# Moving loads against their products in a decoder step: the convolution's input loads and the modulation's weight loads

## The chip, the cores and the metric

One core of one Trainium2 chip. The metric is the device time of one execution in microseconds (us); where several executions of a kernel are shown, their median counts. Engines: TensorE (PE) multiplies, VectorE (DVE), ScalarE (ACT) and GpSimd (POOL) work on elements, SyncE (SP) and POOL issue most transfers.

## The reference, cut to what matters

One layer of a decoder for 256 prompt tokens and 8 x 8 sample tokens (T = 320 tokens in all), in float32. What the change touches is the modulation by a vector c per sequence (6 x 2048 columns) and the convolution of width 31.

```python
ada = silu(c) @ w_ada + b_ada                       # 9 sequences x (6 x 2048)
sh1, sc1, g1, sh2, sc2, g2 = split(ada, 6)
h = layer_norm(x) * (1 + sc1) + sh1
proj = h @ w_in                                     # 2048 -> 7168: u_s, u_c2, gates
y_s = s5_scan(u_s)                                  # state-space branch
br_s = (gelu(y_s) @ w_s5_val) * sigmoid(gelu(y_s) @ w_s5_gate)
u_c = u_c2[:1024] * sigmoid(u_c2[1024:])
v = depthwise_conv(u_c, conv_w, width=31) + conv_b  # convolution branch
br_c = silu(layer_norm(v)) @ w_conv_pw
mix = (g_s * br_s + g_c * br_c) @ w_out
x = layer_norm(ALPHA * x + g1 * mix)
x = layer_norm(ALPHA * x + g2 * moe(layer_norm(x) * (1 + sc2) + sh2))
```

## The kernel before, in words

The program is traced once and a planner (`schedule_with_timeline_sim`) orders each engine's queue when it is built: an instruction's place in the program is its priority, and an instruction that stands further back may go first where the engine would else be idle. On the chip every queue runs in the order so made, and each instruction waits for what it needs.

The stages in time: the first modulation parts with the layer norm and the first 768 columns of `w_in` (until about 182 us), the rest of `w_in`, the products with `w_conv_pw`, `w_s5_val`, `w_s5_gate` and `w_out` (until about 1090 us), the routing, then the experts.

The main products, `gemm` (L551), go by units. A unit is one load of 128 x 1024 weights (512 KB, issued on SP, L557) into one of the four buffers with the tag `raw`, a split of it into a high half (`whi`, ACT, L542) and a low half (`wlo`, DVE, L543), and 24 products of 320 columns (PE, output `acc`; all products stand at line 188, that of the helper). The buffer is free when the low half is made. `run_main` (L920) runs them one ahead: it traces the load of unit n+1, then the products of unit n, then lets the side work go on. Units of interest are counted from the first one behind the 768 columns: 4 units for the rest of u_s, 32 for u_c2, 64 for the gates, then 16 for `w_conv_pw` and 32 for `w_s5_val` and `w_s5_gate`.

Side work is written as generators that yield a cost, and `Side.give` (L582) runs them while their debt is positive. After each main unit `side` (the state-space branch, `s5`) gets 2100, `cside` (the convolution, `conv`, from the first unit of the gates on) gets 1900, and `ada_rest` (the later modulation) gets 1.0.

`conv` (L856) works in 16 blocks, two for each of 8 groups of 128 channels: one of 256 prompt columns, one of 64 sample columns. A block loads four tiles (142 or 151 KB each, issued on POOL, L865, into the free ends of the tiles `s5S` and `s5T`) that hold four shifted copies of the input from the DRAM buffer `up_d`, then runs 64 products into `cv` with the taps in `wide`, which POOL makes once per group (L860), and an activation writes `vf` (L878). The four tiles exist once, so the loads of a block have to wait for the products of the one before.

`ada_set` (L292) makes 1024 columns of the modulation: for each of 8 pairs of rows of `w_ada` it loads two tiles of 512 KB (`ada_load`, issued on SP, L279, in turn) and runs four products into `adp` (eight instructions of PE each time). The tiles come from the same four `raw` buffers, and until the gates' projection begins every second one of most turns from three more (`rawu`, `rawc`). A pair's two buffers are free when its products are done. `ada_rest` runs six such sets (48 pairs) with a cost of 1.3 per yield beside the main units.

Of the kernel before, what the change touches and what calls it, by code (L numbers as in the profile page):

```python
# [19 lines left out]
D = 2048  # L20
# [128 lines left out]
def bc(ap, shape):  # L149
    return ap.to_broadcast(shape)  # L150


def build(tc, A, O):
# [24 lines left out]
    def s5p(name="s5p"):  # L178
        return pp.tile([128, 512], F32, name=name, tag="s5p", bufs=2)

    def tpp(name="tpp"):
        return pp.tile([128, 512], F32, name=name, tag="tpp", bufs=1)

    def stg(name="stg", shape=(128, T), dt=F32):
        return pa.tile(list(shape), dt, name=name, tag="stg", bufs=7)

    def mm(out, l, r, a, b, skip=True):
        return PE.matmul(out, lhsT=l, rhs=r, start=a, stop=b, skip_group_check=skip)  # L188
# [39 lines left out]
    def raw_tile():  # L228
        return pa.tile([128, 1024], F32, name="raw", tag="raw", bufs=4)
# [33 lines left out]
    def four(ops):  # L263

        lead = mm(*ops[0])
        with tc.issue_after(lead.ins), tc.high_priority(offset=3000):
            for x in ops[1:]:
                mm(*x)
# [8 lines left out]
    def in_turn(o, i):  # L277
        with tc.issue_after(turn[0]) if turn else contextlib.nullcontext():
            turn[:] = [SY.dma_start(out=o, in_=i).ins]  # L279

    def ada_load(cols, k):

        i = next(begun) % 8
        raw = more[i // 2] if i % 2 and i < 7 and len(more) else raw_tile()
        if cols[1] == cols[0] + 512:
            in_turn(raw, w_ada[:, k, cols[0]:cols[0] + 1024])
        else:
            for a, c in enumerate(cols):
                in_turn(raw[:, 512 * a:512 * a + 512], w_ada[:, k, c:c + 512])
        return raw  # L290

    def ada_set(cols):  # L292


        ps = pp.tile([128, 512], F32, name="adp", tag="adp", bufs=1)
        for k in range(0, KT, 2):
            raws = [ada_load(cols, k + h) for h in range(2)]
            four([(ps[64 * a + 32 * h:64 * a + 32 * h + 32, :], scT[:, k + h, :], raws[h][:, 512 * a:512 * a + 512],
                   k == 0, k == KT - 2) for h, a in ((1, 1), (0, 0), (0, 1), (1, 0))])
            yield  # L300
            yield
        es = [stg("ae")[:, :256] for i in range(2)]
        for i, e in enumerate(es):
            S.copy(e, ps[:, 256 * i:256 * i + 256])
        yield
        tp = tpp()
        for i in range(4):
            mm(tp[:, 64 * i:64 * i + 64], es[i // 2][:, 128 * (i % 2):128 * (i % 2) + 128], pair, True, True)
        tv = tp[:, :256].rearrange("p (i a s) -> p a i s", i=4, a=2)
        for a, c in enumerate(cols):  # L310
            f = c // 128
            tt(ada[:, f:f + 4, :], tv[:, a, :, :NS], bc(bT[:, f:f + 4, None], [128, 4, NS]), op=OP.add)
        yield
# [309 lines left out]
    for q in range(4):  # L623
        for i, _ in enumerate(ada_set([D + 512 * q, 512 * q])):
            if q == 0:
                if i == 2:
                    x_load()
                    taps()
                if i == 3:
                    bias_rows()  # L630
                    next(norm)
                if 6 <= i < 15:
                    next(norm, None)
                    next(norm, None)
                setup.give(800)
            else:
                if i % 4 == 3 and i < 16:
                    k_outer(4 * q - 4 + i // 4)
                setup.give(1100)
# [216 lines left out]
    def conv():  # L856


        for c in range(8):
            gt(wide, bc(cwS[:, c, :, :, None], [128, 4, 8, 32]), bc(oneh[:, None, None, :], [128, 4, 8, 32]), op=OP.mult)  # L860
            for t0, n, o0, m in ((0, CW - 3 + SEQ, 0, SEQ), (PS, NB * PB - 2, SEQ, NB * TS)):
                xs = [spare[k][:, 1280 + 304 * i:1584 + 304 * i] for k in "TS" for i in range(2)]
                for j, x in enumerate(xs):
                    v = up_d[c, 32 * j:32 * j + 32, t0:t0 + n]
                    GP.dma_start(out=x[:, :n], in_=bass.AP(v.tensor, v.offset, [[1, 4]] + list(v.ap)))  # L865
                yield 3500
                ps, lead = s5p("cv"), None
                for r in range(8):
                    rows = slice(0, 128 if r < 7 else 96)
                    for j in (3, 0, 1, 2):  # L870
                        x = xs[j][rows]
                        if o0:
                            x = x.rearrange("p (b t) -> p b t", b=NB)[:, :, 4 * r:4 * r + TS]
                        else:
                            x = x[:, 4 * r:4 * r + SEQ]
                        with tc.issue_after(lead.ins) if lead else contextlib.nullcontext():
                            lead = mm(ps[32 * j:32 * j + 32, :m], wide[rows, j, r, :], x, r == 0, r == 7)
                S.activation(vf[:, c, o0:o0 + m], ps[:, :m], AF.Identity, bias=vT[:, 8 + c:9 + c])  # L878
                yield 2000

    def conv_norm():
        yield 3000
# [64 lines left out]
    def chain(*gs):  # L947
        for g in gs:
            yield from g
# [29 lines left out]
    def steps(g, cost):  # L979
        for _ in g:  # L980
            yield cost

    ada_rest = Side(steps(chain(*[ada_set([p * D + 1024 * i, p * D + 1024 * i + 512])
                                  for p in (2, 4, 3) for i in range(2)]), 1.3))
    g2s = ada_g2()
    ada_last = Side(steps(g2s, 2.4))
# [8 lines left out]
    for i in range(4):  # L995
        run_main([gemm(w_in, 1024 + 256 * i, KT, *hh, ev_ua), gemm(w_in, 2048 + 256 * i, KT, *hh, ev_ub)], SD, ada_rest,
                 (lambda: side.g.append(s5())) if i == 0 else None)
    more.clear()
    run_main([gemm(w_in, 3072 + 256 * i, KT, *hh, ev_g) for i in range(16)], SD, ada_rest,
             lambda: cside.g.extend((conv(), conv_norm())))  # L1000


# [118 lines left out]
    xr, late = {}, []  # L1121
# [630 lines left out]
    fins, fx, late, lt = {}, [], {}, {}  # L1752
# [250 lines left out]
    cols = ke[:, E_N:E_N + 32]  # L2003
# [280 lines left out]
```

## Time and profile before

| what | value |
|---|---|
| median of three runs | 1654.14 us (1652.2 to 1662.36) |
| the profiled execution | 1669.45 us, its span 1667.7 us |
| PE busy | 1471.1 us, 88% of the span |
| DVE busy | 878.4 us, 53% |
| ACT busy | 551.4 us, 33% |
| POOL busy | 248.2 us, 15% |
| mean granted clock of PE | 0.942 |
| moved by DMA | 447.39 MB, 268 GB/s |

The profile is that of one execution, with every time counted from the start of its span; "idle" of an engine is put down to what ended it. An arrow <- in a wait says who was waited for, in a transfer what is read. "PEclk" is the granted share of PE's full clock.

### The profile page before, as it was taken

The numbers are of one execution on the slowest core, as the hardware profiler recorded it, in microseconds if no ns is written. First come the engines' busy times: TensorE is split into PE (matmuls) and PEld (weight loads), VectorE is DVE, ScalarE is ACT, GpSimd is POOL, SyncE is SP. The second block draws the span as 40 slices with busy tenths as digits, with TensorE's granted clock in tenths as the row PEclk, the third lists the DMA queues.
The fourth block names the chain that finished last, engine by engine and source line by source line (L and its number), as shares of the span: only waits on it lengthen the run. The fifth ranks groups of instructions, "written<-read, shape, count | busy, mean of one in ns | idle before, by whom it ended". The sixth has DMA issues, their size and how long they took to land. (4 is left out here: it accounts for less than half of the span.)

```text
span 1667.7 us, 28096 instructions
## 1 busy us (share of the span) xinstructions
PE 1471.1 (88%) x10731; PEld 1023.4 (61%) x10731; DVE 878.4 (53%) x1724; ACT 551.4 (33%) x960; POOL 248.2 (15%) x419
## 2 busy tenths in 40 slices
PE   4777978998899899989899999988879998969894
PEld 1444967877677777878788988866523332323431
DVE  4744347764834754698345645555531543424365
ACT  1321433342223223632243433323231423232534
POOL 3020212124222220111100100000200000010013
PEclk9886999999999999999899999999999998989997
DMA  9897999779769975876577654567799899999992
GB/s 256 304 312 251 270 270 250 237 190 268 197 200 250 208 199 182 221 231 222 178 253 239 201 161 147 173 209 267 306 403 413 335 413 411 413 356 411 411 412 101
DMA packets 214899, 447.39 MB, mean 268 GB/s; under 512 B 23811, under 2 KB 134067, under 8 KB 206732
## 3 DMA queue, kind: packets, MB, share of 16 engines
q1 hardware_dynamic: 179572, 395.65, 68.3%
q0 software_dynamic: 29168, 43.15, 12.0%
q10 hardware_dynamic: 6016, 6.70, 1.3%
q8 instruction: 87, 1.43, 0.4%
q14 instruction: 56, 0.46, 0.1%
HBM read 425.53 MB, written 21.77 MB: 268 GB/s over the span
## 5 line engine op out<-in xcount | busy, mean ns | idle before, releaser
L543 DVE TENSOR_TENSOR wlo<-raw,whi 128x1024 fp32r<-128x1024 f32 (+1 forms) x196 | 239.8, 1224 | 308.8 <-ACT whi L542 301.1
L542 ACT CAST whi<-raw 128x1024 fp32r<-128x1024 f32 (+1 forms) x196 | 202.2, 1032 | 390.9 <-PE acc L188 253.2
L188 PE MATMUL acc<-h_hi,whi 128*128 128x320 f32 x864 | 276.9, 325 | 5.1 <-ACT whi L542 3.0
L188 PE MATMUL acc<-h_lo,whi 128*128 128x320 f32 x864 | 272.7, 318 | 0.0
L188 PE MATMUL acc<-h_hi,wlo 128*128 128x320 f32 x864 | 261.9, 321 | 6.9 <-DVE wlo L543 6.9
L188 PEld LDWEIGHTS acc<-h_hi,whi 128*128 128x128 f32 x864 | 168.6, 196 | 30.0 <-issue 13.0
L188 PE MATMUL up<-ring,xg 128*32 128x512 f32 x1344 | 176.3, 613 | 8.4 <-PEq L2199 6.5
L188 PEld LDWEIGHTS acc<-h_hi,wlo 128*128 128x128 f32 x864 | 162.9, 194 | 22.7 <-DVE wlo L543 9.4
L188 PEld LDWEIGHTS acc<-h_lo,whi 128*128 128x128 f32 x864 | 168.1, 195 | 3.6 <-issue 1.4
L188 PE MATMUL adp<-raw,scT 128*32 128x512 f32 x636 | 119.0, 685 | 19.4 <-DMA raw<-in_w_ada 19.3
L188 PE MATMUL pd<-ring,aT 128*32 128x512 f32 (+1 forms) x688 | 100.9, 695 | 5.2 <-DVE aT L1872 5.2
L188 PEld LDWEIGHTS up<-ring,xg 128*32 128x32 f32 x1344 | 42.2, 113 | 102.0 <-issue 89.3
L188 PE MATMUL acc<-y_hi,whi 128*128 128x320 f32 x256 | 80.0, 315 | 7.0 <-DVE m L1010 7.0
L1928 ACT COPY z<-pd 32x512 f32<-32x512 f32 (+1 forms) x92 | 53.2, 578 | 90.5 <-PE pd L188 88.0
L1710 DVE TENSOR_TENSOR x1tok<-x1tok,acc 128x512 f32<-128x512 f32 x80 | 51.8, 684 | 55.8 <-PE acc L188 55.5
L188 PE MATMUL acc<-m_hi,whi 128*128 128x320 f32 x256 | 80.6, 316 | 0.0
L188 PE MATMUL acc<-y_lo,whi 128*128 128x320 f32 x256 | 79.5, 312 | 0.0
L188 PE MATMUL acc<-m_lo,whi 128*128 128x320 f32 x256 | 79.4, 311 | 0.0
L188 PE MATMUL acc<-m_hi,wlo 128*128 128x320 f32 x256 | 77.6, 314 | 0.0
L188 PE MATMUL acc<-y_hi,wlo 128*128 128x320 f32 x256 | 75.8, 315 | 0.0
L1611 DVE COPY xg<-XS 128x512 f32 x34 | 14.7, 431 | 85.6 <-PE up L188 82.9
L188 PE MATMUL acc<-vhl,whi 128*128 128x320 f32 x256 | 58.1, 322 | 1.5 <-DVE vhl L915 1.5
(689 smaller groups left out, 2543.2 us busy)
## 6 DMA issues: line engine op xcount, KB each, us to landing
ring<-in_moe_w_up SPq DMA_DIRECT2D x120, 512.0 KB, 11.4
ring<-in_moe_w_gate SPq DMA_DIRECT2D x120, 512.0 KB, 11.6
ring<-in_moe_w_down SPq DMA_DIRECT2D x60, 1024.0 KB, 11.3
raw<-in_w_ada SPq DMA_DIRECT2D x119, 512.0 KB, 5.2
raw<-in_w_in SPq DMA_DIRECT2D x100, 512.0 KB, 5.9
raw<-in_w_ada SPq DMA_DIRECT2D x80, 256.0 KB, 5.4
raw<-in_w_out SPq DMA_DIRECT2D x32, 512.0 KB, 4.4
rawu<-in_w_ada SPq DMA_DIRECT2D x32, 256.0 KB, 5.4
```

The source lines that it names most:

```text
L188: return PE.matmul(out, lhsT=l, rhs=r, start=a, stop=b, skip_group_check=skip)
L542: S.copy(hi[:, :n], raw_ap)
L543: tt(lo[:, :n], raw_ap, hi[:, :n].bitcast(F32), op=OP.subtract)
L1611: state[g % 2] = (V.tensor_copy if g % 2 == 0 else S.copy)(xg[:, :, 32 * g:32 * g + 32], XS[:, :, bass.ds(off, 32)])
L1710: tt(x, x, o, op=OP.add)
L1928: S.copy(zs[q * ng + nb][0][s0:s0 + m_], pd[m_ * q:m_ * q + m_])
```

## The change

`ada_set` gets a flag `late`. With it, the two loads of a pair come first, then a yield, then the products, then the second yield; without it, products follow their loads at once and both yields come behind. The six later sets are run with it. In `conv` the yield between loads and products grows from 3500 to 5500, and the one of 2000 behind the products goes, so that the next block's loads (and the next group's `wide`) are traced straight behind the products. The sum of the costs of a block and of a pair stays.

```diff
-    def ada_set(cols):
+    def ada_set(cols, late=False):
...
             raws = [ada_load(cols, k + h) for h in range(2)]
+            if late:
+                yield
             four([(ps[64 * a + 32 * h:64 * a + 32 * h + 32, :], scT[:, k + h, :], raws[h][:, 512 * a:512 * a + 512],
                    k == 0, k == KT - 2) for h, a in ((1, 1), (0, 0), (0, 1), (1, 0))])
-            yield
+            if not late:
+                yield
             yield
...
                     GP.dma_start(out=x[:, :n], in_=bass.AP(v.tensor, v.offset, [[1, 4]] + list(v.ap)))
-                yield 3500
+                yield 5500
                 ps, lead = s5p("cv"), None
...
                 S.activation(vf[:, c, o0:o0 + m], ps[:, :m], AF.Identity, bias=vT[:, 8 + c:9 + c])
-                yield 2000
...
-    ada_rest = Side(steps(chain(*[ada_set([p * D + 1024 * i, p * D + 1024 * i + 512])
+    ada_rest = Side(steps(chain(*[ada_set([p * D + 1024 * i, p * D + 1024 * i + 512], True)
                                   for p in (2, 4, 3) for i in range(2)]), 1.3))
```

## Rows read from the trace of the kernel before

**Rows 1.** The page: busy us (share of the span) and instructions of each engine.
```profile
PE 1471.1 (88%) x10731; PEld 1023.4 (61%) x10731; DVE 878.4 (53%) x1724; ACT 551.4 (33%) x960; POOL 248.2 (15%) x419
```
**Rows 2.** Stretches: length; PE, PEld, DVE, ACT, POOL busy; clock; DMA share; GB/s.
```profile
182.00:370.00 188.00, 167.72 (x1096) 149.76 (x1096) 112.31 (x162) 69.12 (x121) 44.72 (x84) 0.95 0.89 250
370.00:655.00 285.00, 262.34 (x2377) 213.59 (x2375) 161.54 (x232) 84.58 (x129) 82.51 (x104) 0.96 0.87 215
655.00:930.00 275.00, 257.48 (x1709) 229.74 (x1708) 169.52 (x272) 109.59 (x168) 28.14 (x56) 0.97 0.70 221
```
**Rows 3.** Waits of PE, 182 to 370 us: us in total, times, longest.
```profile
PE acc L188 <- DVE wlo L543: 5.7, 4, 2.1
PE adp L188 <- DMA raw<-in_w_ada: 4.6, 1, 4.6
PE adp L188 <- DMA rawc<-in_w_ada: 4.3, 2, 3.2
PE adp L188 <- DMA rawu<-in_w_ada: 3.2, 3, 2.1
```
**Rows 4.** Waits of PE, 370 to 655 us.
```profile
PE cv L188 <- DMA s5S<-up_d: 12.4, 6, 4.1
PE cv L188 <- DMA s5T<-up_d: 3.6, 3, 2.0
PE adp L188 <- DMA raw<-in_w_ada: 3.2, 2, 1.7
...
PE acc L188 <- DVE wlo L543: 0.8, 1, 0.8
```
**Rows 5.** Waits of PE, 655 to 930 us.
```profile
PE adp L188 <- DMA raw<-in_w_ada: 4.2, 4, 1.4
PE acc L188 <- DVE wlo L543: 3.2, 2, 2.8
```
**Rows 6.** The stretch behind the longest cv wait, columns as in rows 2.
```profile
575.60:582.60 7.00, 6.94 (x29) 6.07 (x29) 4.59 (x16) 0.00 (x0) 0.00 (x0) 0.51 0.75 220
```
**Rows 7.** Waits of POOL, 370 to 655 us: us in total, times, longest.
```profile
POOL s5S L865 <- PE cv L188: 131.6, 13, 15.8
```
**Rows 8.** POOL in order of time: start, us, what [idle before <-releaser].
```profile
446.81 0.68 POOL L865 DMA_DIRECT2D s5S<-up_d  x1 [11.85 <-PE cv L188]
...
450.97 0.68 POOL L865 DMA_DIRECT2D s5S<-up_d  x1
```
**Rows 9.** Instructions of acc in two stretches: length, PE busy (xcount), and on.
```profile
182.60:441.00 258.40, 195.35 (x1200) 184.70 (x1200) 2.50 (x6) 12.87 (x30) 0.96 0.92 245
182.60:575.60 393.00, 285.50 (x1751) 267.83 (x1751) 2.50 (x6) 18.15 (x42) 0.97 0.92 237
```
**Rows 10.** PE in order of time: cv of block 3 behind its wait.
```profile
441.01 0.30 PE L188 MATMUL cv<-s5T,wide 128*32 128x64 f32 x2 [2.02 <-DMA s5T<-up_d]
```
**Rows 11.** Transfers, 370 to 655 us: KB each, median us to landing.
```profile
raw<-in_w_in SPq DMA_DIRECT2D x47, 512.0 KB, 5.9
...
s5T<-up_d POOLq DMA_DIRECT2D x16, 151.0 KB, 7.8
```
**Rows 12.** Instructions of acc between a freed load and its product (as rows 9).
```profile
856.30:867.40 11.10, 10.19 (x68) 9.93 (x68) 0.00 (x0) 0.88 (x2) 1.00 0.74 232
```
**Rows 13.** PE in order of time: one group of adp.
```profile
855.26 1.07 PE L188 MATMUL adp<-raw,scT 128*32 128x512 f32 x8
```
**Rows 14.** Waits of SP, 182 to 930 us: us in total, times, longest.
```profile
SPq L557 <- PE adp L188: 79.6, 29, 7.5
...
SPq L279 <- PE adp L188: 20.8, 10, 3.2
```
**Rows 15.** The split (busy us, mean ns) and a load (KB, us), 740 to 930 us.
```profile
L543 DVE TENSOR_TENSOR wlo<-raw,whi 128x1024 fp32r<-128x1024 f32 x43 | 52.8, 1227 | 53.1 <-ACT whi L542 50.8 <-PE tpp L188 2.2
...
L542 ACT CAST whi<-raw 128x1024 fp32r<-128x1024 f32 x42 | 44.0, 1049 | 79.4 <-PE acc L188 70.1 <-DMA raw<-in_w_conv_pw 9.3
...
raw<-in_w_s_val SPq DMA_DIRECT2D x16, 512.0 KB, 4.3
```

## The prediction

> **What bounds the kernel.** I read the page first: TensorE (PE) is busy 88% of the span, no other engine much over half of it [rows 1]. Then the table by stage, since both edits act only between about 182 and 930 us, where the projections run: there PE is busy 89 to 94% of each stretch, VectorE 57 to 62% [rows 2]. So in these stages PE sets the end: an idle microsecond of PE there is a microsecond of the kernel, while idle time of SP and POOL, which only issue loads, costs nothing until a product waits for a load. Last I read what ended PE's idle time in each of the three stretches, and three causes matter here:
> - the modulation's products (adp) wait for their rows of w_ada: 4.6 + 4.3 + 3.2 = 12.1 us in 182 to 370, 3.2 in 370 to 655, 4.2 in 655 to 930, so 19.5 us in 12 waits [rows 3 to 5];
> - the convolution's products (cv) wait for their inputs from up_d: 12.4 + 3.6 = 16.0 us in 9 waits, all in 370 to 655 [rows 4];
> - the main products (acc) wait for the low half of their own weights: 5.7 + 0.8 + 3.2 = 9.7 us [rows 3 to 5].
>
> A stall can cost more than itself: after the longest cv wait (4.1 us) the granted clock of the next 7 us was 0.51, the lower level of 1.2 GHz, which gave away about 3.4 us [rows 6]. All that the change speaks of is thus 19.5 + 16.0 us and some 5 us of clock, out of 1654.
>
> **Part one, the convolution.** Nothing is added or removed: the same 16 blocks of four loads, one activation and 64 products. In the program the loads of block h+1 stood 2000 cost units, about one main unit (1900), behind the products of block h, and now stand right behind them; the products are now 5500 behind their loads instead of 3500. But the queue order is made by the planner, which fills an idle queue with whatever can go. Does the queue already do it? POOL waited 131.6 us in 13 waits for cv products, with the loads of the next block at its head [rows 7]: in 13 of 16 blocks the loads are already queued directly behind the products. In the block shown, the first load goes out at 446.81, in the instant that the products release it (a wait of 11.85 us ends), and the four are out by 451.65 [rows 8]. The edit can take no lead from a queue that is already waiting.
>
> What of the other half, products that come later? The cost of 1900 per main unit puts block 3 (counted from 0) behind 47 units of main products (24 each, counted from 182.6 us) and block 11 behind 70; the new costs put them behind 48 and 71. Executed were 1200/24 = 50.0 units when block 3 had to wait, until 441.0, and 1751/24 = 73.0 when block 11 had the longest wait of all, until 575.6 [rows 9, 10]. So where they stall, the products stand 3 units behind their old place and 2 behind the new one; what places them is when the planner thinks that the load is there, and the new cost does not hold them back. The loads take up to 7.8 us to land [rows 11], and all 9 waits are the rest of that. Term: 0. Its bounds are 0 and -16.0, with -3.4 of clock; I take the end at 0, because the queue row is nearest to the edit. What stands behind the loads on POOL (the state-space branch's own loads) meets the same waiting queue as now. The activation and POOL's multiply move with the products and are hidden as before: ACT and POOL are idle most of this stretch [rows 2].
>
> The Trainium skill, "DMA: Bandwidth & Descriptors", section "Anatomy of one DMA — SWDGE (gpsimd) path", fits a POOL-issued load as 2.0 us plus its bytes over 436 GB/s, an estimate of 2.3 us for 151 KB. By that price every load would be in before its product and this term could be nothing but 0; the trace has 7.8 us [rows 11], so there is a wait to win, and only the order says that it is not won.
>
> **Part two, the modulation.** Six sets of eight pairs, 48 pairs of 512-KB loads, each with four products. Issue and number stay; the pair's products go one step (1.3 main units) later in the program, behind the next main unit. Three things follow.
>
> Gain: a main unit is 24 products; 68 of them took 11.1 us with one group of adp (1.07 us) among them, so (11.1 - 1.07)/68 = 147 ns each and 3.5 us a unit [rows 12, 13]. Each of the 12 waits can be covered up to 3.5 us by the unit put in front: 18.4 of the 19.5 us. But 12.1 of them lie where the DMA engines are 89% busy [rows 2] and main products wait for their weights too (5.7 us [rows 3]): there part of the wait only passes to the next product. And part of the groups stand where PE had nothing else to do: the planner will put them there again. I take -10, about half, between 0 and -18.4.
>
> Loss: a pair's two buffers are freed by its products, so they come free up to a unit later, and there are only four "raw" buffers, shared with the main weights (seven until the gates' projections begin). SP, which issues all of these in order, waits for adp 29 times (79.6 us) with a main load at its head and 10 times (20.8 us) with the next pair [rows 14]. What is late next is therefore a main load, and all that is queued behind it. Take the load that adp freed at 856.3: its product began at 867.4, a lead of 11.1 us [rows 12]. It needs the landing (4.3 us there, 5.9 for w_in [rows 11, 15]), the cast to the high half (1.05) and the subtraction (1.23) [rows 15]: 6.6 to 8.2 us. With adp a unit later the lead is 11.1 - 3.5 = 7.6: enough by 1.0 us, or short by 0.6. So the loss lies between 0 and 29 x 0.6 = 17 us. I take +4: in the later stretch the load is quick, in the earlier ones the leads are mostly longer.
>
> Hidden: the copies and additions that end a set move by less than a unit, and their results are first read in the output projection. The first "wide" on POOL shares a buffer with one of these pairs and may start a unit later; POOL is busy 45 of 188 us there [rows 2]. Term: -10 + 4 = -6.
>
> **Sum.** The profiled execution took 1669.45 us (span 1667.7 and 1.75 around it), 15.3 above the median of 1654.14. Its sum is 1669.45 + 0 - 6 = 1663.5; against the median, 1648.
>
> **Rivals.**
> - *It does what its words say* (faster). The loads do gain a unit: all 16.0 us of cv waits go, the clock gives 3.4, adp gives 10 and nothing is lost: 1654 - 29 = 1625. For it: every cv wait is for a landing. Against it: the queue is already there [rows 7], and the products stall behind their new place [rows 9, 10]. It would need the planner to put the products elsewhere because the loads moved.
> - *The buffers starve the main products* (slower). Leads of 7.6 us where 8.2 are needed: +17, and no gain, since a pair that must wait for its predecessor's buffers gets no lead either: 1671. It decides from the point where the main load's lead falls under landing plus split. For it: SP's 39 waits on adp [rows 14]. Against it: main products waited for weights only 9.7 us in all this time [rows 3 to 5], so there is slack now. The Trainium skill, "Perfetto Trace Analysis", section "Optimization Strategy", says that a gap which repeats on the engine that should be saturated can mean too few buffers for the next tile; by it, holding buffers longer is the wrong direction. The rows agree that it is buffers that SP waits for, and show no such gap on PE so far.
> - *The edit does nothing* (same). The planner hoists the moved products back into the places where PE is idle: 1654.
>
> **Chances.** Forecast (a small gain, 1638 to 1660) 0.36, nothing (1648 to 1662) 0.16, faster 0.28, slower 0.20. The order of every queue is made anew, so each may be off by some microseconds. A measurement of this kernel tells about 1% (16 us: the three runs lie 10 us apart). The first two cases lie within 1%, the third over it; of the slower case's 0.20 I leave 0.02 within 1%, since its price ends there. That makes faster 0.28, same 0.54, slower 0.18. The range 1624 to 1671 reaches to both rivals' times and leaves out about a tenth on either side; the likeliest case alone has 1638 to 1660.
>
> **What would show it.** Right: waits of cv for up_d stay near 16 us and POOL still waits over 100 us for cv; waits of adp for w_ada after 182 us fall from 19.5 to about 10; waits of acc for the low half rise from 9.7 by a few us; SP's waits for adp grow. Wrong: cv waits under 5 us (first rival), acc waits for the low half over 25 us (second), or adp waits unchanged (third). It would also be wrong if the new order moved the state-space branch's work, which I took as unmoved.

## The result and the profile after

The changed kernel takes 1675.74 us (median of 11 runs, 1667.82 to 1687.88), the kernel before 1657.8 beside it (11 runs, 1648.47 to 1674.18). The ratio is 1.0099, 95% interval 1.0072 to 1.0127: 16.4 us slower, where 6 us faster was predicted and the range ended at 1671. (The ratios of this document are those on record, of fast runs alone, and not quotients of two medians, here 1.0108; 16.4 us is 0.99% of 1657.8.) The profiled execution took 1680.58 us, 11.1 more than that of before.

The table by stage of the changed kernel, columns as in [rows 2]:

```profile
182.00:370.00 188.00, 171.30 (x1109) 151.43 (x1109) 114.82 (x165) 68.98 (x121) 44.53 (x85) 0.95 0.90 252
370.00:655.00 285.00, 261.12 (x2332) 209.70 (x2332) 156.68 (x228) 83.81 (x128) 76.23 (x103) 0.95 0.87 210
655.00:930.00 275.00, 255.56 (x1690) 226.34 (x1689) 168.34 (x266) 108.06 (x166) 26.94 (x52) 0.98 0.69 221
```

In the middle stretch PE is nearly as busy as before (261.12 us of 285; 262.34 in [rows 2]), but did 2332 products in it instead of 2377. What PE waited for from 182 to 936 us in the changed kernel (us in total, times, longest), beside the sums of [rows 3 to 5]:

```profile
PE cv L188 <- DMA s5S<-up_d: 13.6, 5, 4.8
PE adp L188 <- DMA raw<-in_w_ada: 12.5, 5, 4.5
PE acc L188 <- DVE wlo L546: 9.2, 9, 1.9
PE acc L188 <- ACT whi L545: 6.9, 6, 2.7
...
PE adp L188 <- DMA rawc<-in_w_ada: 3.8, 2, 2.0
PE adp L188 <- DMA rawu<-in_w_ada: 2.9, 3, 2.3
```

The waits of adp are 19.2 us, against 19.5: the whole gain that was forecast isn't there. The main products wait 16.1 us for the two halves of their own weights; before it was 9.7 for the low half [rows 3 to 5] and 1.2 for the high one (182 to 930 us):

```profile
PE acc L188 <- ACT whi L542: 1.2, 1, 1.2
```

And cv waits 13.9 us (13.6 for s5S and 0.3 for s5T; 16.0 before). POOL, and then SP (182 to 930 us), as in [rows 7] and [rows 14]:

```profile
POOL s5S L868 <- PE cv L188: 143.2, 11, 17.1
```

```profile
SPq L560 <- DMA raw<-in_w_in: 53.3, 17, 8.7
SPq L279 <- PE adp L188: 48.7, 16, 6.2
SPq L560 <- PE adp L188: 46.6, 21, 6.9
```

POOL waits for cv as it did. SP's wait for adp has moved: with a main load at its head it fell from 79.6 to 46.6 us, with the next modulation pair at its head it rose from 20.8 to 48.7 [rows 14]. And with a main load at its head SP waited 53.3 us for an earlier main load to land, where it was 21.0 before:

```profile
SPq L557 <- DMA raw<-in_w_in: 21.0, 14, 3.2
```

**Where the 11.1 us are.** Units of 24 main products are counted from here on from the first of them all, as in the expectations below, which is 8 more than in the prediction. From the start of unit 16 to that of unit 160 (a row by stage for each kernel, before and after):

```profile
218.20:960.20 742.00, 683.95 (x5170) 589.80 (x5168) 451.72 (x694) 262.76 (x412) 145.17 (x225) 0.97 0.80 221
```

```profile
216.80:966.70 749.90, 691.86 (x5169) 592.24 (x5167) 451.22 (x694) 263.03 (x412) 138.62 (x225) 0.96 0.79 218
```

This stretch is 7.9 us longer, and PE's idle time in it is the same: 742.00 - 683.95 = 58.05 and 749.90 - 691.86 = 58.04. The same products took 7.9 us longer. By the clock's record PE ran 51.2 us of this stretch at the lower level before, and 64.9 us after; 13.7 us at half speed give away 6.9. Of the rest of the 11.1, 4.4 us are in the last 150 us of the experts' stage (150.9 to 155.3; 10.3 and 20.5 us at the lower level), and the start is 1.4 shorter. The edits change nothing in the experts' stage: all that stands behind unit 160 takes between 706 and 716 us in the 20 traces of this document, whatever the edit.

This pair isn't typical. Of the eleven timed runs of the kernel before, one was slower than its profiled execution of 1669.45 us. Two kernels that time like it, with profiled executions near its median, have less idle time and less low clock in this stretch: pace_2120 (49.8 and 37.5 us) and before_stg4 (52.2 and 47.7), both described below. Beside these two the changed kernel's stretch is 13.9 to 19.3 us longer, with 5.8 to 8.2 us more idle time and 17 to 27 us more at the lower level. So it is idle time and clock, not the clock alone.

What such a low stretch looks like: the first follows the stall that ends at 393.56, the second begins within the 4.83 us for which cv waits until 616.71 (columns as in [rows 2]; the clock is third from the end).

```profile
394.32:397.73 3.41, 3.41 (x14) 3.10 (x13) 3.04 (x4) 1.45 (x3) 2.52 (x5) 0.50 0.50 151
616.19:626.43 10.24, 9.72 (x83) 6.89 (x84) 1.23 (x1) 1.18 (x2) 0.09 (x1) 0.50 0.27 81
```

In the first PE is busy throughout, at 0.50 of its clock (1.2 of 2.4 GHz): 14 products in 3.41 us, 244 ns each instead of 147 [rows 12].

**One stall in full.** SP, ACT and PE of the changed kernel in order of time (start, us, what [idle before <-releaser]):

```profile
380.08 2.33 SPq L279 DMA_DIRECT2D raw<-in_w_ada  x2
382.51 1.23 SPq L560 DMA_DIRECT2D raw<-in_w_in  x2
```

```profile
380.96 1.06 PE L188 MATMUL adp<-raw,scT 128*32 128x512 f32 x8
```

```profile
392.47 1.04 ACT L545 CAST whi<-raw 128x1024 fp32r<-128x1024 f32 x1 [5.97 <-DMA raw<-in_w_in]
```

```profile
393.56 0.41 PE L188 MATMUL acc<-h_hi,whi 128*128 128x320 f32 x1 [2.73 <-ACT whi L545]
```

The pair's second load goes out at 382.07, when the adp products in front, begun at 380.96, free its buffer, and the main load of unit 50 stands behind it on SP's queue and follows at 382.51. It lands at 392.4, 9.9 us later, is cast, and PE has stood for 2.73 us. From issue to first product this load has a lead of 393.56 - 382.51 = 11.05 us; the same load had 14.9 in the kernel before, where that adp group stands at 373.40 and the pair behind it is out by 376, and it was not waited for. But PE stood in those 14.9 us as well, 4.1 us in two other waits:

```profile
387.92 0.64 PE L188 MATMUL adp<-raw,scT 128*32 128x512 f32 x4 [1.69 <-DMA raw<-in_w_ada]
395.24 0.64 PE L188 MATMUL s5p<-us,Bs 128*128 128x320 f32 x1 [2.40 <-ACT Wre L760]
```

So a stall here is in part the exchange of one for another. Over the 48 main loads of units 48 to 96 the median lead fell from 16.2 to 14.9.

### The profile page after: what moved, and what is told of

Read it like the earlier page. It is cut to its first block, busy times and chain, and to the rows that moved or that the text cites. A ratio compares the mean times of both kernels' runs of the same rounds, so it can differ in the third digit from the quotient of the medians.

```text
span 1678.8 us, 28106 instructions
## 1 busy us (share of the span) xinstructions
PE 1483.6 (88%) x10731; PEld 1029.7 (61%) x10731; DVE 879.0 (52%) x1724; ACT 551.4 (33%) x960; POOL 241.8 (14%) x419
## 5 line engine op out<-in xcount | busy, mean ns | idle before, releaser
L188 PEld LDWEIGHTS acc<-h_hi,whi 128*128 128x128 f32 x864 | 169.8, 198 | 36.0 <-ACT whi L545 15.7
L188 PE MATMUL pd<-ring,aT 128*32 128x512 f32 (+1 forms) x688 | 96.9, 670 | 5.2 <-DVE aT L1874 5.2
L1613 DVE COPY xg<-XS 128x512 f32 x34 | 14.7, 431 | 85.8 <-PE up L188 83.3
## 6 DMA issues: line engine op xcount, KB each, us to landing
ring<-in_moe_w_down SPq DMA_DIRECT2D x60, 1024.0 KB, 11.3
```

Of the source, the lines that this page charges most:

```text
L1613: state[g % 2] = (V.tensor_copy if g % 2 == 0 else S.copy)(xg[:, :, 32 * g:32 * g + 32], XS[:, :, bass.ds(off, 32)])
```

## The experiments

The theory formed on these traces (A): the modulation's later products hold their raw buffers longer, what is queued on SP behind the next pair is late, and main products stall on their own weights. Rivals: B, the convolution's edit does it; C, any new order moves the time by as much; I, the harm lies in the places that the new order gives to cv and adp. Two more, for two of the runs: P, the harm sits at one place along the kernel; S, each set of the modulation costs a little.

All results first. "16 to 160" is the length of the stretch in the profiled execution; idle, low clock, and the wait of adp (from unit 8) are in us; "own" is the wait of main products for their own weights in units 48 to 96, and "lead" the median from issue to first product of the main loads there. Each trace is one execution: where a kernel was traced twice, the stretch differs by 3.4 to 3.9 us.

| kernel | ratio (95%) | 16 to 160 | idle | low clock | adp | own | lead |
|---|---|---|---|---|---|---|---|
| before | 1 | 742.0 | 58.1 | 51.2 | 19.5 | 0.8 | 16.2 |
| changed | 1.0099 (1.0072 to 1.0127) | 749.9 | 58.0 | 64.9 | 19.2 | 5.2 | 14.9 |
| after_again | 1.0069 (1.0033 to 1.0105) | 746.5 | 56.3 | 61.5 | 18.6 | 3.6 | 14.8 |
| conv_only | 0.9994 (0.9967 to 1.0022) | 730.1 | 49.9 | 40.9 | 19.8 | 3.2 | 16.0 |
| ada_only | 1.0035 (1.0006 to 1.0064) | 736.3 | 54.9 | 40.9 | 17.4 | 7.4 | 14.5 |
| ada_only_2 | 1.0025 (0.9984 to 1.0067) | 732.4 | 49.2 | 47.7 | 16.9 | 5.0 | 14.4 |
| pace_2120 | 0.9986 (0.9946 to 1.0027) | 730.6 | 49.8 | 37.5 | 23.0 | 0.6 | 15.7 |
| late_12 | 1.0032 (1.0001 to 1.0063) | 732.7 | 50.4 | 44.3 | 14.7 | 6.0 | 14.6 |
| late_not12 | 1.0036 (1.0008 to 1.0064) | 739.5 | 54.8 | 58.0 | 18.0 | 0.3 | 16.1 |
| late2 | 1.0020 (0.9989 to 1.0052) | 735.1 | 53.8 | 44.3 | 14.3 | 5.2 | 13.1 |
| after_5000 | 1.0090 (1.0061 to 1.0119) | 750.7 | 60.2 | 61.4 | 24.9 | 4.1 | 15.2 |
| after_6000 | 0.9979 (0.9946 to 1.0013) | 742.1 | 54.7 | 44.5 | 26.0 | 0.9 | 14.7 |
| conv_6000 | 0.9971 (0.9940 to 1.0003) | 721.5 | 43.6 | 27.2 | 17.2 | 1.9 | 14.8 |
| before_stg4 | 1.0001 (0.9974 to 1.0028) | 736.0 | 52.2 | 47.7 | 13.6 | 0.4 | 15.8 |
| before_raw5 | 0.9971 (0.9937 to 1.0005) | 725.1 | 47.9 | 34.0 | 10.5 | 0.2 | 20.8 |
| conv_raw5 | 0.9967 (0.9939 to 0.9996) | 715.8 | 39.9 | 30.6 | 8.7 | 0.6 | 19.8 |
| after_raw5 | 0.9933 (0.9903 to 0.9964) | 719.2 | 36.8 | 44.3 | 6.2 | 0.5 | 20.2 |
| ada_raw5 | 0.9896 (0.9849 to 0.9944) | 712.4 | 34.8 | 30.6 | 4.4 | 0.9 | 20.2 |
| ada_raw5_2 | 0.9895 (0.9861 to 0.9929) | 716.3 | 38.7 | 27.2 | 6.2 | 0.7 | 20.5 |
| raw5_6000 | 0.9934 (0.9906 to 0.9962) | 717.0 | 39.6 | 30.6 | 4.4 | 3.8 | 18.7 |

### Each edit alone, a neutral re-ordering, and the changed kernel again

conv_only takes only the two changes in `conv`, ada_only only the modulation's. pace_2120 is the kernel before with

```
-    PACE = dict(s5=2100, conv=1900)
+    PACE = dict(s5=2120, conv=1900)
```

> Only the convolution's edit (loads directly behind the products, 5500 units to the next products). The changed kernel was 16 us slower than before (ratio 1.010). Theory A, the modulation's edit holds buffers longer and does the harm: this kernel stays within 5 us of before (ratio 0.997 to 1.003), since the loads were queued directly behind the products already; waits of cv for its inputs stay between 12 and 18 us. Theory B, the convolution's edit does the harm (its products come at other places): ratio about 1.010 and the modulation's edit alone near 1.000. Theory C, any new order costs or gives some microseconds: 1.003 to 1.007 for this one and for the neutral one alike.

> Only the modulation's edit (the products one step behind their loads). Theory A: ratio about 1.010, main products' waits for their own weights (whi and wlo) after 182 us 14 to 18 us as in the changed kernel (10.9 before), waits of adp near 19. Theory B: ratio near 1.000. Theory C: 1.003 to 1.007. The prediction's own step had this edit alone at -6 us (0.996).

> A neutral change: none of the two edits; the state-space branch is given 2120 instead of 2100 units per main unit (1% more), so that the planner's order changes from about unit 84 on (some 77 products of adp, cv and s5p stand up to 2 units elsewhere) while no buffer is held longer on purpose. Theory A and B: ratio 0.998 to 1.002. Theory C (any re-ordering moves the time): away from 1.000 by more than 0.003, to either side, with the granted clock's low stretches after 182 us changed from about 55 us.

> The changed kernel once more, beside the others on the same chip: 1.010 (1.007 to 1.013) by what was measured. In its trace the stretch from the first main unit to 1080 us should again have about the same idle time of TensorE as before (61 against 61.6 us) and about 14 us more at the lower clock; if instead the low stretches come out as before's, the clock is no part of the cause.

The convolution's edit alone doesn't move the time (0.9994), so B falls. Its waits of cv were to stay at 12 to 18 us and were 6.4: that expectation missed. PE's idle time in all is still that of pace_2120 (49.9 and 49.8 us), whose cv waits were 10.3. The modulation's edit alone costs 0.35%, and 0.25% the second time (an interval that holds 1): a third to a half of what both cost together, and not the 1.010 that A had written down. The neutral re-ordering stays at 0.9986, so C isn't what the 0.7 to 1.0% are, though the neutral one's interval of 0.4% to either side covers the small differences here. The changed kernel again ran 61.5 us of units 16 to 160 at the lower clock. In ada_only the waits of main products for their weights are the longest of its list (182 to 920 us):

```profile
PE acc L188 <- DVE wlo L546: 13.6, 13, 2.2
...
PE acc L188 <- ACT whi L545: 6.4, 5, 3.5
```

That is A's sign, 20.0 us where before had 10.9; in the second trace it is 15.9.

> The modulation's edit alone once more (1.0035 at first), since the open point is a difference of 0.5% between it and both edits together (1.0099 and 1.0069). If the edits' costs do not add (the convolution's new places cost only with the modulation's), 1.001 to 1.005 again, and its trace has no stall of cv at unit 56.6. If the first time was too fast and the modulation's edit makes all the harm, 1.006 to 1.010.

The second time bears the first out: the costs of the two edits don't add up to that of both.

### Where along the kernel

late_12 moves the modulation's products in the second and third set only, late_not12 in the others (both with the convolution's edit):

```
-    ada_rest = Side(steps(chain(*[ada_set([...], True)
+    ada_rest = Side(steps(chain(*[ada_set([...], (p, i) in ((2, 1), (4, 0)))
```

> The changed kernel, but the modulation's products a step later only in the second and third of the six sets (units 44 to 72 of the main products); the other four sets as before. Its order is the changed kernel's up to unit 82 and the kernel before's from there. Theory P (the place: both traces of the changed kernel have stalls at units 49.9 for whi and 56.6 for cv that neither edit alone shows, and 31 us of low clock in units 48 to 96 against 7 to 20): ratio 1.005 to 1.010, and both stalls are there. Theory S (spread: each set costs a little wherever it stands): a third to a half of the harm, 1.002 to 1.004.

> The complement: the convolution's edit, and the modulation's products a step later in the first, fourth, fifth and sixth set alone. Its order is that of the convolution's edit alone up to unit 72, the changed kernel's from there. Theory P: ratio 0.998 to 1.003, no stall at units 49.9 and 56.6. Theory S: 1.004 to 1.007.

1.0032 and 1.0036: each half carries about half of the harm (0.7 to 1.0%), which speaks for S, though the second lies just under the 1.004 to 1.007 that S had. The stalls of the changed kernel at units 49.9 and 56.6 are in late_12's trace too (2.75 and 1.75 us) and not in late_not12's, so they are not the whole harm.

### A fifth raw buffer

A fifth raw buffer (4 KB a partition) has room when four of the small staging buffers are kept instead of seven:

```
-        return pa.tile(list(shape), dt, name=name, tag="stg", bufs=7)
+        return pa.tile(list(shape), dt, name=name, tag="stg", bufs=4)
...
-        return pa.tile([128, 1024], F32, name="raw", tag="raw", bufs=4)
+        return pa.tile([128, 1024], F32, name="raw", tag="raw", bufs=5)
```

> The kernel before with five raw buffers instead of four (paid with four small staging buffers instead of seven). Control for the next. Between 0.990 and 1.005 of before: adp waits (19.5 us) should fall if buffers are what delays their loads; the staging buffers may cost some.

> The changed kernel with the same five raw buffers and four staging buffers. Theory A (the harm comes from buffers that the modulation's pair holds a unit longer): its ratio is within 0.003 of the control's, since the fifth buffer takes up the longer hold. Theory I (the harm comes from where the new order puts the products of cv, adp and the main unit): 0.006 to 0.012 over the control's.

> The kernel before with four staging buffers instead of seven and four raw buffers as ever: the control for the controls. If the fifth raw buffer gave the 0.3% of the control with five, this one stands at 0.999 to 1.004; if it was the staging buffers (by another order), 0.995 to 0.998.

> The modulation's edit alone, with five raw buffers and four staging buffers. The kernel before with these stood at 0.9971, the changed one at 0.9933. Theory A: the modulation's edit gives all of that difference, so 0.992 to 0.995, with waits of adp after 182 us near 6 us (10.5 in the control). If the convolution's edit gave it, 0.996 to 0.999.

> The convolution's edit alone with five raw and four staging buffers (control 0.9971; modulation's edit alone 0.9896; both 0.9933). If the two edits add up, 1.000 to 1.003: the convolution's edit then costs 0.004 when the modulation's is there and about 0.003 without. If it is neutral as with four buffers (0.9994), 0.995 to 0.999, and the modulation's edit alone with five buffers was measured somewhat too fast.

> The modulation's edit alone with five raw and four staging buffers once more: the fastest version, with only six timed executions so far (0.9896). If the convolution's edit costs 0.4% beside the modulation's there too, 0.987 to 0.991; if it is neutral there, 0.992 to 0.995 as with both edits (0.9933).

This experiment tells most. With four buffers the changed kernel stands 0.7 to 1.0% above before; with five the harm is gone: it stands 0.4% below its control (0.9933 against 0.9971, with intervals that overlap), and the modulation's edit alone 0.75% below it, twice (0.7 and 0.4% by the medians). The staging buffers alone do nothing (1.0001). A fifth buffer also makes the order of the queues anew, so places change with it; what goes with the buffers is the lead, 18.7 to 20.8 us in all six traces with five and 13.1 to 16.2 in all with four. PE's waits in the control (182 to 906 us), in the changed kernel with five buffers (182 to 912 us), and in ada_raw5_2 (182 to 909 us):

```profile
PE adp L188 <- DMA raw<-in_w_ada: 9.1, 5, 6.2
PE acc L188 <- ACT whi L542: 7.9, 6, 2.9
PE acc L188 <- DVE wlo L543: 7.3, 9, 2.9
...
PE adp L188 <- DMA rawc<-in_w_ada: 1.1, 1, 1.1
```

```profile
PE acc L188 <- ACT whi L545: 6.7, 6, 2.4
PE adp L188 <- DMA raw<-in_w_ada: 6.2, 8, 2.2
PE acc L188 <- DVE wlo L546: 6.1, 8, 2.5
```

```profile
PE adp L188 <- DMA raw<-in_w_ada: 4.3, 5, 1.3
...
PE adp L188 <- DMA rawc<-in_w_ada: 1.9, 1, 1.9
```

Now adp waits 6.2 us where the control waits 10.5, and the main products lose nothing by it in units 48 to 96 (0.5 us; 5.2 with four buffers), with leads of 20.2 us there. But most of what adp gains is one wait, that of the pair behind unit 108, in the control and in the changed kernel with five buffers:

```profile
709.31 1.08 PE L188 MATMUL adp<-raw,scT 128*32 128x512 f32 x4 [6.20 <-DMA raw<-in_w_ada]
```

```profile
718.59 1.08 PE L188 MATMUL adp<-raw,scT 128*32 128x512 f32 x4 [2.25 <-DMA raw<-in_w_ada]
```

In ada_raw5 and ada_raw5_2 this wait is 0.8 and 0.9 us; all the others of the control add up to 4.3. The stretch from unit 16 to 160 of ada_raw5_2:

```profile
222.60:938.90 716.30, 677.56 (x5156) 581.83 (x5155) 450.00 (x689) 262.69 (x409) 138.21 (x225) 0.98 0.82 229
```

At 1645.1 us against 1658.76 (a ratio of 0.9895 on record, 0.9918 as quotient of the medians) the modulation's edit with five raw buffers is faster than both kernels. Where along the kernel its 0.75% lie the traces don't tell: conv_raw5 has the same stretch (715.8 us) and stands at 0.9967.

### More of the same, and other places

late2 puts the products two steps behind their loads (the second yield, behind the products until now, goes in front of them); after_5000, after_6000 and conv_6000 change the convolution's 5500, and with it the cost of a block; raw5_6000 is the fifth buffer with 6000.

```
             if late:
                 yield
+                yield
```

```
-                yield 5500
+                yield 6000
```

> The dose doubled: the changed kernel with the modulation's products two steps behind their loads instead of one. In its order some 17 of the 48 pairs stand up to 2 units later than in the changed kernel. Theory A (a pair that holds its buffers longer delays the main loads behind it): ratio 1.010 to 1.020, main products' waits for their own whi and wlo after 182 us over 20 us (16 in the changed kernel, 11 before), waits of adp under 15 (19). Theory I (places of the new order alone): 1.003 to 1.010, with no trend in the waits.

> The changed kernel with the convolution's products 6000 units behind their loads instead of 5500: its blocks stand 0.5 to 6 units later, so that the second block no longer stands at unit 54 (the changed kernel has a stall of cv there at unit 56.6 in each trace), and nothing changes in how long the modulation's pairs hold their buffers. If the convolution's edit adds to the harm by the place of that block, 1.000 to 1.005; if the harm is the buffers' alone, 1.005 to 1.010. Waits of cv for its inputs (14 us) should fall under 8 if later products can outlast their loads, as the change's words want.

> The changed kernel with 5000 instead of 5500 units: the first two of the 16 convolution blocks' groups stand where they stand in the changed kernel (units 46 and 54), the later ones up to 4.6 units earlier. If the stall at the second group (unit 56.6) with its clock makes the harm, 1.006 to 1.010 as in the changed kernel; if it is the places of the later groups, it goes to 0.998 to 1.004.

> The convolution's edit alone with 6000 instead of 5500 units: the control of the changed kernel with 6000 (0.9979). If the modulation's edit harms by holding buffers wherever the convolution stands, this one is 0.003 to 0.009 faster than that (0.989 to 0.995) and its main products wait under 3 us for their own weights in units 48 to 96. If the harm belonged to the changed kernel's own places of the blocks, it stands within 0.002 of it (0.996 to 1.000).

> Both edits, 6000 units, five raw and four staging buffers: the version that should gain from both. If what 6000 gave with four buffers (-0.010) and the fifth buffer (-0.014) add up, 0.983; if they remove the same stalls, 0.989 to 0.994.

Here A misses. Two steps should have cost more and cost less (1.0020). Its leads fell again, to 13.1 us, and main products waited 20.2 us for their weights in all, as A has it; but adp waited 5 us less (14.3), cv waited 9.4, and the low clock was 44.3 us. PE's list of late2 (182 to 924 us) begins with

```profile
PE acc L188 <- DVE wlo L547: 12.2, 10, 2.8
PE acc L188 <- ACT whi L546: 8.0, 6, 1.9
```

With the convolution 500 units later the modulation's edit costs next to nothing (0.9979 against 0.9971, where A had 0.3 to 0.9% between them), below both ranges written down for it. In units 48 to 96 its main products hardly wait (0.9 us), but over the whole of it they wait 17.4 us and adp 26.0, so the waits don't say why; what is lower than in the changed kernel is the low clock (44.5 us) and, by little, the idle time (54.7). Nor does the lead decide it alone: conv_6000, without the modulation's edit, has 14.8 us. With 500 units less the harm is there in full (1.0090), with the same two stalls at units 49.9 and 56.6 (2.75 and 3.12 us). So I holds too: with four buffers the edit makes main loads late, and where cv and adp stand goes into what that costs. raw5_6000 shows that the two remedies don't add (0.9934), as if they removed the same stalls; its main products still waited 3.8 us in units 48 to 96, so that isn't shown.

**All traces together.** One trace of each kernel says little, but there are enough for two groups with four buffers: five without the modulation's edit (before, conv_only, pace_2120, conv_6000, before_stg4) and seven with the whole of it (changed, after_again, ada_only, ada_only_2, late2, after_5000, after_6000). From 182 us to unit 160, the main products' waits for their own weights are 10.9 to 14.7 us without and 15.9 to 20.2 with it, and the two ranges don't meet. With five buffers they do: 15.2 and 17.0 without, 13.3 to 18.7 with it. In the mean of the two groups the stretch is 9.9 us longer with the edit (732.0 and 741.9), the idle time 4.6 more (50.7 and 55.3) and the low clock 11.3 more (40.9 and 52.2), which gives away 5.6, though in these three the groups overlap; adp waits no less (18.6 and 19.6). That is A's chain, with the clock paying about as much as the stalls.

**What stays open.** Why the two edits together cost 0.4 to 0.7% more than the modulation's alone, with four buffers and with five (0.9933 against 0.9895). The row that goes with it is the lower clock (61 to 65 us in the three traces near 1.01, 41 to 48 in ada_only's two; with five buffers 44 against 31 and 27), but late_12 has the changed kernel's order up to unit 82 and ran only 10 us of units 48 to 96 at the lower level, where the changed kernel ran 31 in both of its traces. What makes that difference at the same order wasn't found.

## Why the prediction was wrong, step by step

- **What bounds the kernel**: right. PE's idle time and clock are where the time went.
- **The convolution's term, 0**: right in time for the edit alone (0.9994; with five buffers 0.9967 against 0.9971), and in what it was read from, POOL's wait of 143.2 us for cv. That all 16.0 us of cv's waits would stay was right for both edits together (13.9) and not for this one alone: 6.4 in conv_only, 6.5 in conv_raw5 where the control has 12.6. And the 16.0 us of [rows 4], taken as what is there to win, were one execution's: the same order up to unit 84 had 10.3 in pace_2120.
- **The modulation's gain, -10**: the step that failed first. It counted 3.5 us of lead for each wait and took half of the 18.4 as won. Measured 0.3 (adp 19.2 for 19.5) and, alone, 2 to 3 us. The lead is won only where the planner moves the product, and it left 33 of the 48 pairs within a fifth of a unit of their old place on PE's queue (12 stand about 1 to 2 units later, 3 about one earlier). In the 15 that moved the mechanism is as forecast: from the issue of the second load to the first product they have 27.4 us in the mean instead of 24.8, and their two waits of before, 3.2 us at 387.92 and 415.28, are gone, in after_again and ada_only too. But the other 15.5 us of the six sets' waits, all of theirs between 182 and 370 us among them, stood in the 33 pairs that stayed, and those wait 19.0 us now (0.7 us of the 19.5 belong to an earlier set). Of the 19.0, 4.5 us are at one place where nothing waited before. A wait that went, in the kernel before, and the one that came, in the changed kernel:

```profile
415.28 0.64 PE L188 MATMUL adp<-raw,scT 128*32 128x512 f32 x4 [1.51 <-DMA raw<-in_w_ada]
```

```profile
514.11 1.08 PE L188 MATMUL adp<-raw,scT 128*32 128x512 f32 x4 [4.51 <-DMA raw<-in_w_ada]
```

  That the planner would put groups back was written down, and half was taken off for it and for what passes on; it was five sixths for this alone. And the next pair's loads wait for the buffers that the moved products hold: SP's wait with the next pair at its head rose from 20.8 to 48.7 us. With a fifth buffer the edit gave 0.4 to 0.75%, about the size that was forecast or above, but not shown to come from the lead: adp's waits are 10.5 us there without any edit, and what the edit takes of them is nearly one wait.
- **The modulation's loss, +4**: right in kind and in size as a wait: 10.9 to 16.1 us, +5.2. The leads behind it fell by 1.3 us in the median and by 3.9 for the load of unit 50. But the load shown to come short isn't one that adp frees, as in the working at 856.3 [rows 12]; it is the load behind the next pair, and it took 9.9 us to land, not the 4.3 to 5.9 of the sum. Those were medians: in the kernel before, of the 33 main loads from 370 to 655 us whose landing is on record, 7 took over 9 us.
- **The term that was missing: the clock.** The prediction wrote down that a stall can cost more than itself [rows 6], put "some 5 us of clock" at stake where, from unit 16 to 160, 51.2 us at the lower level gave away 25.6, and then charged new stalls at their length. In the profiled pair the idle time is equal to 0.1 us, and the lower clock makes 6.9 of the 7.9 us; in the mean of all traces with four buffers it makes about half.
- **The sum of two edits taken by themselves**: wrong. 0.9994 and 1.0035 don't make 1.0099.
- **What was taken as unmoved**: the state-space branch's work did move, which the prediction had named as a sign of being wrong. From unit 8 on, 17 of its 96 products s5p stand half a unit to 2 units elsewhere on PE's queue in the changed kernel and in ada_only, none in conv_only. What that cost was not separated.
- **The rivals**: "the buffers starve the main products" had the sign and, by the fifth buffer, the cause in the main, with a chance of 0.20. That its 17 us are close to the measured 16.4 is luck: they were to be waits for weights, over 25 us in all, and 16.1 showed, with the clock beside them. "Adp waits unchanged", named as the sign of the third rival, came true as well, and for that rival's reason: the planner left the products that waited where they were. The Trainium skill, "Perfetto Trace Analysis", section "Optimization Strategy", holds that a gap repeating on the engine that should be saturated can mean too few buffers; the prediction set it aside because PE showed no such gap. The fifth buffer agrees with the page: 0.9971 for the kernel before (0.9937 to 1.0005, so hardly clear of 1), and with the modulation's edit 0.75% less.

## What to carry to other kernels

Where a planner orders the queues, look first which of the waiting products an edit will in fact move: here the 15 pairs that moved had 3.2 us of the 19.5. What a product gains by standing further behind its load it takes from its buffer; with a pool this tight, count the buffers first, and try one more before moving anything. In a queue issued in order, look at what stands behind the load that will now wait, not at that load. Price every new stall of the bound engine with the slower stretch that follows it, not with its length alone, and price a load that is nearly late by its slow landings, not by the median. And don't take one profiled execution for the kernel: that of before was among its slowest, and what seemed equal beside it (PE's idle time) was not.

## What the hardware showed

A single stall in an engine busy for over 90% of the time went with 3.4, 6.8 or 10.2 us at the lower clock, and its length doesn't tell which: at unit 86.4 the 3.88 us of cv in ada_only went with 3.4, the 4.83 in the changed kernel with 10.2; the 1.91 us at unit 74.5 in ada_only went with none. Over units 16 to 160 this came to 27 to 65 us in kernels that run the same products. The landing of one 512-KB load of w_in, 5.9 us in the median [rows 11], was 9.9 us for the load of 382.51, with two other 512-KB loads going out in the 2.5 us before it and one 0.9 us behind it.
